# Modulation weights as the stationary operand, and the first weight tile multiplied channel by channel, in the opening of a hybrid diffusion layer

## The chip, the cores and the metric

The kernel runs on one core of one Trainium2 chip. The metric is device time in microseconds (us), from one launch of the whole program. A core has a matrix engine (PE in the profile, with its weight loads shown apart as PEld), a vector engine (DVE), a scalar engine (ACT), GpSimd (POOL), and SyncE (SP), which here only starts transfers.

## The reference, cut to what matters

The layer has 256 context tokens and 2048 latent tokens of 1024 channels. Only its first step matters here:

```python
ml = split_mod(jax.nn.silu(c) @ w_mod[layer] + b_mod[layer])            # 1 x 1024 @ 1024 x 6144
mc = split_mod(jax.nn.silu(c_ctx)[None] @ w_mod[layer] + b_mod[layer])
hl = modulate(rmsnorm(xl, g_norm1[layer]), ml[0], ml[1])                # h * (1 + scale) + shift
hc = modulate(rmsnorm(xc, g_norm1[layer]), mc[0], mc[1])
pl = split_proj(hl @ w_in[layer])                                       # 1024 x 3600
pc = split_proj(hc @ w_in[layer])
```

So a shift and a scale for each of 1024 channels, for two conditioning vectors, must exist before any token can be projected. After that come a bidirectional mLSTM and a short convolution over the tokens, an output projection, a routed mixture of 16 experts, and a final norm.

## The kernel before

The kernel works through the latent tokens in four blocks of 512. For each block it normalises and modulates the tokens, transposes them so that channels lie on the 128 partitions (eight channel groups, k = 0 to 7), and multiplies by `w_in` in tiles of 256 columns. Every projected value is made of three products, because weights and tokens are split into a rounded high part and a low remainder: high times high, high weight times low token, low weight times high token.

The opening is what comes before the first weight tile can be multiplied. Its parts, by name and line:

- **The queue of loads.** Lines 209 to 236 start the loads, most of them on SP's queue, which keeps their order. `wm_load(q)` (L219) brings quarter q of the shift and scale columns of `w_mod`: two tiles of 1 MiB, r = 0 for shift and r = 1 for scale. The order is quarter 0, two context tiles (`cxt`, 512 KiB each), quarter 1, two token tiles (`xt`, 512 KiB each), quarter 2, two token tiles, quarter 3. Behind them come the weight tiles of `w_in`, started by `load_w` (L84). Three loads go by POOL's queue: `gbb`, `ghb` (L131, L133) and `wg` (L276).
- **Buffers.** The quarters 1 to 3 lie in the three `whi` and three `wlo` buffers (pool `whip`) which later hold the split weights. Quarter 0 lies in one `wraw` buffer and in the buffer of `KT`. `split_w` (L89) makes the high part on ACT (L93, `whi`) and the low part on DVE (L97, `wlo`).
- **The modulation** (L248 to L267). For each quarter and each r, eight k-steps multiply the two conditioning vectors `lc` (stationary, 128x2) by 256 columns of `wm` (moving) into `pr` (L255). In the profile each float32 product is two PE instructions, here called passes. DVE copies the two rows out (L257, `mrow`), and two small transposes (L259) put them on partitions in `pm`. Three DVE instructions (L261 to L265) make `B1` and `A1`.
- **Token preparation.** `prep_x` (L154) normalises a tile; `prep_k` (L170) transposes channel group k of all tiles of a set (L176, `pt`), and ACT and DVE make its high and low parts `hhi` and `hlo` (L183 to L187). In the loop over quarters the context runs with quarter q and the tokens one quarter behind.
- **The first products.** `wstat` (L411) multiplies one half of a weight tile (i = 0 or 1) by all eight k into one PSUM bank (`ps`, L417 to L419). The first tile of `w_in` is that of columns 2048 to 2303 (here called tile 1), the next one tile 2; both serve the keys, for the context (256 columns moving) and for the first block (512 columns moving). Results are copied by ACT into `KTc` (L555) and `KT` (L558). PSUM pools: `pmm` has four banks, `ptr` two, `psm` two.

The order on each engine is not the program's: a planner with its own timeline and costs places the instructions of each engine, and the engine then runs its own list strictly in that order.

Of the kernel before, what the change touches and what calls it, by code (L numbers as in the profile page):

```python
# [8 lines left out]
F32 = mybir.dt.float32  # L9
# [10 lines left out]
P = 128  # L20
D = 1024
KD = D // P
SEQ = 2048
NCTX = 256
# [14 lines left out]
def kernel(ctx, tc, x, c, cx, c_ctx, w_mod, b_mod, g_norm1, g_norm2, w_in, w_out, conv_w, conv_b,  # L39
                       gate_b, g_head, w_router, w_gate_e, w_up_e, w_down_e, g_final, out):  # L40
    nc = tc.nc
    V, S, G, T = nc.vector, nc.scalar, nc.gpsimd, nc.tensor
# [3 lines left out]
    w_in = w_in[0]  # L46
# [16 lines left out]
    ident = con.tile([P, P], F32, name="ident")  # L63
# [20 lines left out]
    def load_w(src, rows, cols):  # L84
        raw = wrawp.tile([P, rows, cols], F32, name="wraw", tag="wraw")
        nc.sync.dma_start(raw, src)
        return raw

    def split_w(raw, rows, cols, after=None, after_lo=None):  # L89
        hi = whip.tile([P, rows, cols], F32R, name="whi", tag="whi")  # L90
        if after is not None:
            S.activation(hi[:, 0, 0:1], after, AF.Copy)
        S.activation(hi, raw, AF.Copy)  # L93
        lo = whip.tile([P, rows, cols], F32R, name="wlo", tag="wlo")
        if after_lo is not None:
            tc.keep_in_program_order(G.tensor_copy(lo[:, 0, 0:1], after_lo))
        V.tensor_sub(lo, raw, hi.bitcast(F32))  # L97
        return hi, lo

    vcol = con.tile([P, 96], F32, name="vcol")  # L100
    lc = con.tile([P, KD, 2], F32, name="lc")
# [26 lines left out]
    MB = con.tile([P, NCH + 1, NH], F32, name="MB")  # L128
    Cb0 = con.tile([P, NH, P + 1], F32, name="Cb0")
    gbb = con.tile([P, 16], F32, name="gbb")  # L130
    nc.gpsimd.dma_start(gbb, gate_b.rearrange("o a b -> o (a b)").broadcast_to([P, 16]))  # L131
    ghb = con.tile([P, 512], F32, name="ghb")
    nc.gpsimd.dma_start(ghb, g_head.rearrange("o a b -> o (a b)").broadcast_to([P, 512]))  # L133

    low = ghb[:, 0:2 * P]
    top = ghb[:, 2 * P:3 * P].bitcast(I16)
# [7 lines left out]
    def pool(st, name, bufs, **kw):  # L144
        return st.enter_context(tc.tile_pool(name=name, bufs=bufs, reuse_waits="tile", **kw))

    hp = pool(left, "hT", 12)
    wl = pool(left, "p1l", 2)
    pmm = pool(left, "p1mm", 4, space=PSUM)
    wk = pool(right, "p1e", 2, side="right")  # L150
# [19 lines left out]
    def prep_k(xn, k, s, h, st):  # L170
        his, los = h
        nt = len(xn)
        ntok = nt * P
        pt = ptr.tile([P, 512], F32, name="pt", tag="tr")
        for t in range(nt):
            T.transpose(pt[:, t * P:(t + 1) * P], xn[t][:, k * P:(k + 1) * P], ident)  # L176
        if ntok == 512 or k % 2 == 0:
            st[0] = hp.tile([P, 512], F32R, name="hhi", tag="hhi")
            st[1] = hp.tile([P, 512], F32R, name="hlo", tag="hlo")
        o_ = 0 if ntok == 512 else (k % 2) * ntok  # L180
        hi = st[0][:, o_:o_ + ntok]
        lo = st[1][:, o_:o_ + ntok]
        S.activation(hi, pt[:, :ntok], AF.Identity, scale=A1[:, k, s:s + 1], bias=B1[:, k, s:s + 1])  # L183
        hf = wl.tile([P, 512], F32, name="hf", bufs=2)
        V.tensor_scalar(hf[:, :ntok], pt[:, :ntok], A1[:, k, s:s + 1], B1[:, k, s:s + 1],
                        op0=ALU.mult, op1=ALU.add)
        V.tensor_sub(lo, hf[:, :ntok], hi.bitcast(F32))  # L187
        his.append(hi)
        los.append(lo)
# [9 lines left out]
    wms = []  # L199
# [19 lines left out]
    def wm_load(q):  # L219
        for r in range(2):  # L220
            o_ = r * D + q * 256
            nc.sync.dma_start(wms[q * 2 + r], w_mod[:, o_:o_ + 256].rearrange("(k p) n -> p k n", p=P))

    wm_load(0)
    cxt = [ml2b, ml5b]
    for t in range(2):
        nc.sync.dma_start(cxt[t], cx[t * P:(t + 1) * P, :])
    wm_load(1)
    xn = []
    for t in range(4):  # L230
        xt = wk.tile([P, D], F32, name="xt", bufs=4)
        nc.sync.dma_start(xt, x[t * P:(t + 1) * P, :])
        xn.append(xt)
        if t == 1:
            wm_load(2)
    wm_load(3)
    lcr = wk.tile([16, P], F32, name="lcr", tag="Kt", bufs=2)
    S.activation(lcr, vrow[0:16, :], AF.Silu)
    pv = psm.tile([P, 512], F32, name="pv", tag="sm")
# [6 lines left out]
    prep_x(None, 4, xn)  # L246
    hc, stc = ([], []), [None, None]
    h, sth = ([], []), [None, None]  # L248
    for q in range(4):
        pmf = psm.tile([P, 512], F32, name="pm", tag="sm")  # L250
        pm = pmf[:, 0:8].rearrange("p (r i s) -> p r i s", r=2, i=2)
        for r in range(2):
            pr = pmm.tile([P, 512], F32, name="pr", tag="mm")
            for k in range(KD):
                T.matmul(pr[:2, :256], lc[:, k, :], wms[q * 2 + r][:, k, :], start=k == 0, stop=k == KD - 1)  # L255
            mrow = wk.tile([2, 256], F32, name="mrow", tag="cm" if r else "ur", bufs=1)
            V.tensor_copy(mrow, pr[:2, :256])  # L257
            for i in range(2):
                T.transpose(pm[:, r, i], mrow[:, i * P:(i + 1) * P], ident[:2, :2])  # L259
        sl = slice(q * 2, q * 2 + 2)  # L260
        V.tensor_tensor(B1[:, sl], pm[:, 0], vcol[:, 16 + q * 2:18 + q * 2].unsqueeze(2).to_broadcast([P, 2, 2]),  # L261
                        op=ALU.add)
        V.tensor_tensor(A1[:, sl], pm[:, 1], vcol[:, 24 + q * 2:26 + q * 2].unsqueeze(2).to_broadcast([P, 2, 2]),
                        op=ALU.add)
        V.scalar_tensor_tensor(A1[:, sl], A1[:, sl], 1.0,  # L265
                               vcol[:, 64 + q * 2:66 + q * 2].unsqueeze(2).to_broadcast([P, 2, 2]),
                               op0=ALU.add, op1=ALU.mult)  # L267
        for k in (q * 2, q * 2 + 1):
            prep_k(cxn, k, 1, hc, stc)
        if q:  # L270
            for k in (q * 2 - 2, q * 2 - 1):
                prep_k(xn, k, 0, h, sth)
    for k in range(6, KD):
        prep_k(xn, k, 0, h, sth)
    wg = wl.tile([P, KD, 16], F32, name="wg", bufs=1)
    nc.gpsimd.dma_start(wg, w_in[:, 3584:3600].rearrange("(k p) n -> p k n", p=P))  # L276
    wgp = wl.tile([P, 2, KD, 32], F32R, name="wgp", bufs=1)
    zr = wl.tile([P, KD, 16], F32, name="zr", bufs=1)
    V.memset(zr, 0.0)
# [127 lines left out]
    def wtile(n0):  # L407
        raw = load_w(w_in[:, n0:n0 + 256].rearrange("(k p) n -> p k n", p=P), KD, 256)
        return split_w(raw, KD, 256)

    def wstat(w, i, h, ntok):  # L411
        hi, lo = w
        his, los = h
        ps = pmm.tile([P, 512], F32, name="ps", tag="mm")
        for k in range(KD):
            wh = hi[:, k, i * P:(i + 1) * P]
            T.matmul(ps[:, :ntok], wh, his[k], start=k == 0, stop=False)  # L417
            T.matmul(ps[:, :ntok], wh, los[k], start=False, stop=False)  # L418
            T.matmul(ps[:, :ntok], lo[:, k, i * P:(i + 1) * P], his[k], start=False, stop=k == KD - 1)  # L419
        return ps  # L420
# [127 lines left out]
    for blk in range(4):  # L548
        KT = wk.tile([P, NH, 512], F32, name="KT", bufs=1)
        for j in range(2):  # L550
            w = wtile(2048 + j * 256)
            if blk == 0:
                for i in range(2):
                    ps = wstat(w, i, hc, NCTX)
                    S.activation(KTc[:, j * 2 + i, :], ps[:, :NCTX], AF.Copy)  # L555
            for i in range(2):
                ps = wstat(w, i, h, 512)
                S.activation(KT[:, j * 2 + i, :], ps, AF.Copy)  # L558
        if blk == 0:
            pv = psm.tile([P, 512], F32, name="pv", tag="sm")  # L560
# [3 lines left out]
        for j in range(2):  # L564
            w = wtile(2560 + j * 256)
            if blk == 0:
                for t in range(2):
                    ps = hstat(w, hc, t)
                    V.tensor_copy(V1c[t][:, j * 2:j * 2 + 2, 0:P], ps[:, :256].rearrange("p (h v) -> p h v", h=2))
            for t in range(4):  # L570
                if j == 0:
                    V.memset(V1s[t][:, :, P:P + 1], 1.0)
                ps = hstat(w, h, t)
# [8 lines left out]
        for j in range(2):  # L582
            w = wtile(1536 + j * 256)
            for i in range(2):
                ps = wstat(w, i, h, 512)
# [60 lines left out]
        for j in range(2):  # L646
            mod_tile(j)
            w = wtile(3072 + j * 256)
            for t in range(4):
                so = wl.tile([P, 256], F32, name="so", bufs=2)  # L650
                ps = hstat(w, h, t)
# [4 lines left out]
        for j in range(2):  # L656
            mod_tile(2 + j)
            cs = []
            w = wtile(512 + j * 256)
            for i in range(2):  # L660
                ps = wstat(w, i, h, 512)
# [3 lines left out]
            w = wtile(1024 + j * 256)  # L665
            ys = []
            for i in range(2):
                ct = j * 2 + i
                ps = wstat(w, i, h, 512)
# [11 lines left out]
            w = wtile(j * 256)  # L681
            for i in range(2):
                ct = j * 2 + i
                y = ys[i]
                ps = wstat(w, i, h, 512)
# [3 lines left out]
        h = hnext  # L689

    left.close()
    wk = pool(left, "p2", 2)
# [137 lines left out]
    for n_, k2 in enumerate((2, 3, 0, 1)):  # L830
        raw = load_w(w_out[k2 * 2 * P:(k2 + 1) * 2 * P, :].rearrange("(k p) n -> p k n", p=P), 2, D)
        if n_ < 3:
            hi = whip.tile([P, 2, D], F32R, name="whi", tag="whi")
            lo = whip.tile([P, 2, D], F32R, name="wlo", tag="wlo")
        else:
            hi = wk.tile([P, 2, D], F32R, name="whi3", bufs=1)
            lo = wk.tile([P, 2, D], F32R, name="wlo3", bufs=1)
# [70 lines left out]
    with tc.tile_pool(name="rt", bufs=1, reuse_waits="tile") as rt, tc.tile_pool(name="rtp", bufs=2, space=PSUM, reuse_waits="tile") as rtp:  # L908
# [82 lines left out]
        r = RB[:, 0].rearrange("p (a q) f -> p a q f", a=2)  # L991
# [5 lines left out]
    with tc.tile_pool(name="xw", bufs=2, reuse_waits="tile") as xraw, tc.tile_pool(name="xh", bufs=2, reuse_waits="tile") as xhi, \  # L997
# [159 lines left out]
        for e in range(NE):  # L1157
# [4 lines left out]
            for pr in range(npair):  # L1162
                n = 2 if pr < npair - 1 else NFT - 2 * (npair - 1)
# [22 lines left out]
                for i in range(n):  # L1186
                    ps = pmm.tile([P, 2, 2 * P], F32, name="psx", tag="mm")
                    for m_ in range(2):
                        hi, lo = ws[m_]
                        for k in range(KD):  # L1190
                            wh = hi[:, k, i * P:(i + 1) * P]
# [85 lines left out]
```

## Time and profile before

| what | value |
|---|---|
| median of 3 runs | 2697.55 us (2696.11 to 2704.61) |
| the profiled execution, its own time | 2698.35 us |
| its span, first to last instruction | 2696.3 us |
| PE busy | 2615.3 us, 97% of the span |
| PEld busy | 2365.0 us, 88% |
| DVE busy | 1584.3 us, 59% |
| ACT busy | 1155.3 us, 43% |

The span lies 2.05 us under the time of its own execution, and that time 0.8 us over the median of the runs. Busy time of PE is modelled at its ends and overlaps; the distance from one PE start to the next tells more.

### The profile page before, as it was taken

To read this page: it belongs to the slowest core of one execution; us is meant where nothing else is said; L and a number is where in the kernel's file an instruction comes from. 1 tells how busy PE (TensorE), PEld (TensorE's weight loads), DVE (VectorE), ACT (ScalarE), POOL (GpSimd) and SP (SyncE) were. 2 spreads that over 40 slices of the span, in tenths; PEclk is the share of its full clock that TensorE was granted. 3 is DMA by queue.
4 is the path that set the end of the run, shared out by engine and by line. 5 is a ranking of instruction groups with operands and counts; after the bars stand their busy time and mean duration, and the time that the engine had idled before them with its cause. 6 is when DMAs were issued, how large, how long until landed. Compare 5 with 4: busy or idle time off the path is not lost.

```text
span 2696.3 us, 42922 instructions
## 1 busy us (share of the span) xinstructions
PE 2615.3 (97%) x17570; PEld 2365.0 (88%) x17570; DVE 1584.3 (59%) x2570; ACT 1155.3 (43%) x1723; POOL 301.0 (11%) x345
## 2 busy tenths in 40 slices
PE   8999999999999999689999999999999999999997
PEld 4988888888878888579999999999999999999987
DVE  5356454554575665566566556656655665665684
ACT  3243333422534444354444444444444444444553
POOL 1010000000111111210011011001101100110231
PEclk9999999999999999889999999999999999999999
DMA  8444554645656655165666666666666666666894
GB/s 271 135 147 148 170 165 147 196 129 156 204 183 206 208 183 172 64 219 188 205 217 208 200 209 219 189 208 214 209 202 208 219 191 206 214 210 202 276 318 166
DMA packets 382532, 524.57 MB, mean 195 GB/s; under 512 B 15072, under 2 KB 322736, under 8 KB 380288
## 3 DMA queue, kind: packets, MB, share of 16 engines
q1 hardware_dynamic: 327968, 437.96, 50.0%
q10 hardware_dynamic: 43792, 46.55, 5.1%
q0 software_dynamic: 10576, 37.32, 5.0%
q8 instruction: 138, 2.26, 0.3%
q14 instruction: 58, 0.48, 0.1%
HBM read 449.05 MB, written 72.61 MB: 193 GB/s over the span
## 4 chain that ended last, share of the span: by engine, by line
PE 63%; DMA 3%; DVE 2%; issue 2%; ACT 0%; POOL 0%; POOLq 0%; DVEq 0%; SPq 0%; ACTq 0%
PE psx L1192 12%; PE psx L1194 11%; PE psx L1193 11%; PE ac L1117 6%; PE ac L1119 6%; PE ac L1118 6%; PE po L730 2%; PE po L732 2%; PE po L731 2%; DMA pk<-PK 1%; PE ptx L1055 1%; PE pl L766 1%; PE pb L514 1%; PE pa L510 1%; DMA ACC<-yv,idx 1%
## 5 line engine op out<-in xcount | busy, mean ns | idle before, releaser
L1192 PE MATMUL psx<-xh,whi 128*128 128x256 f32 x2816 | 788.9, 281 | 1.6 <-ACT whi L93 1.5
L1193 PE MATMUL psx<-xl,whi 128*128 128x256 f32 x2816 | 786.7, 280 | 0.9 <-DVE xl L1064 0.9
L1194 PE MATMUL psx<-xh,wlo 128*128 128x256 f32 x2816 | 787.5, 280 | 0.0
L97 DVE TENSOR_TENSOR wlo<-wraw,whi 128x2048 fp32r<-128x2048 f32 x248 | 532.0, 2156 | 307.8 <-ACT whi L93 304.7
L93 ACT ACTIVATE whi<-wraw 128x2048 fp32r<-128x2048 f32 x248 | 446.7, 1804 | 373.3 <-PE psx L1193 112.1
L1194 PEld LDWEIGHTS psx<-xh,wlo 128*128 128x128 f32 x2816 | 535.3, 190 | 0.1
L1193 PEld LDWEIGHTS psx<-xl,whi 128*128 128x128 f32 x2816 | 530.5, 188 | 3.3 <-DVE xl L1064 1.4
L1192 PEld LDWEIGHTS psx<-xh,whi 128*128 128x128 f32 x2816 | 528.7, 188 | 4.1 <-ACT whi L93 1.7
L1117 PE MATMUL ac<-dhi,hh 128*128 128x512 f32 x704 | 276.2, 392 | 0.0
L1118 PE MATMUL ac<-dlo,hh 128*128 128x512 f32 x704 | 274.7, 390 | 0.0
L1119 PE MATMUL ac<-dhi,hl 128*128 128x512 f32 x704 | 273.3, 390 | 0.0
L1077 DVE TENSOR_TENSOR dlo<-draw,dhi 128x2048 fp32r<-128x2048 f32 x96 | 202.9, 2114 | 114.2 <-ACT dhi L1075 114.2
L418 PE MATMUL ps<-hlo,whi 128*128 128x512 f32 (+1 forms) x672 | 259.6, 387 | 0.0
L419 PE MATMUL ps<-hhi,wlo 128*128 128x512 f32 (+1 forms) x672 | 259.0, 386 | 0.0
L417 PE MATMUL ps<-hhi,whi 128*128 128x512 f32 (+1 forms) x672 | 258.6, 388 | 0.0
L1147 POOL DMA_INDIRECT ACC<-yv,idx x28 | 82.8, 2956 | 1124.1 <-DVE yv L1142 1012.6
L1075 ACT ACTIVATE dhi<-draw 128x2048 fp32r<-128x2048 f32 x96 | 170.2, 1772 | 69.7 <-PE ac L1119 67.6
L1201 ACT ACTIVATE hh<-sgt 128x256 fp32r<-128x256 f32 x176 | 73.2, 417 | 263.0 <-DVE sgt L1197 263.0
L1196 ACT ACTIVATE sgt<-psx 128x256 f32<-128x256 f32 x176 | 65.4, 372 | 228.0 <-PE psx L1194 227.9
L1119 PEld LDWEIGHTS ac<-dhi,hl 128*128 128x128 f32 x704 | 132.1, 188 | 27.8
L428 PE MATMUL ps<-whi,hhi 128*128 128x256 f32 x544 | 156.0, 287 | 0.0
L429 PE MATMUL ps<-wlo,hhi 128*128 128x256 f32 x544 | 154.9, 285 | 0.0
(411 smaller groups left out, 3901.8 us busy)
## 6 DMA issues: line engine op xcount, KB each, us to landing
wraw<-in_w_gate_e_dram SPq DMA_DIRECT2D x80, 1024.0 KB, 6.2
wraw<-in_w_up_e_dram SPq DMA_DIRECT2D x80, 1024.0 KB, 5.5
draw<-in_w_down_e_dram SPq DMA_DIRECT2D x80, 1024.0 KB, 6.1
wraw<-in_w_in_dram SPq DMA_DIRECT2D x56, 1024.0 KB, 5.5
pk<-PK SPq DMA_DIRECT2D x16, 1284.0 KB, 7.7
xt<-in_x_dram SPq DMA_DIRECT2D x32, 512.0 KB, 5.5
wraw<-in_w_mod_dram SPq DMA_DIRECT2D x16, 1024.0 KB, 6.8
wm<-in_w_mod_dram SPq DMA_DIRECT2D x8, 1024.0 KB, 12.0
```

The lines of the kernel that those rows point to most:

```text
L93: S.activation(hi, raw, AF.Copy)
L97: V.tensor_sub(lo, raw, hi.bitcast(F32))
L417: T.matmul(ps[:, :ntok], wh, his[k], start=k == 0, stop=False)
L418: T.matmul(ps[:, :ntok], wh, los[k], start=False, stop=False)
L419: T.matmul(ps[:, :ntok], lo[:, k, i * P:(i + 1) * P], his[k], start=False, stop=k == KD - 1)
L1077: V.tensor_sub(lo, raw, hi.bitcast(F32))
L1117: T.matmul(ac, hhs, dh[:, i, sl], start=f == 0, stop=False)
L1118: T.matmul(ac, hhs, dl[:, i, sl], start=False, stop=False)
L1119: T.matmul(ac, hls, dh[:, i, sl], start=False, stop=f == NFT - 1)
L1192: T.matmul(ps[:, m_], wh, xh[:, k], start=k == 0, stop=False)
L1193: T.matmul(ps[:, m_], wh, xl[:, k], start=False, stop=False)
L1194: T.matmul(ps[:, m_], lo[:, k, i * P:(i + 1) * P], xh[:, k], start=False, stop=k == KD - 1)
```

## The change

The quarter's products swap operands: 128 columns of `wm` become the stationary operand and the two vectors of `lc` the moving one, so that the result lands on partitions in `pm` at once; `pr`, the copies `mrow` and the small transposes go away. The order of the loads becomes quarters 0 and 1, context, all four token tiles, weight tile 1 (`raw0`), quarters 2 and 3, then `wg`, `gbb` and `ghb` on SP's queue. Four PSUM banks are held from the opening on for tile 1, two for the context and two for the tokens. Once quarter 1 is done, tile 1 is split, and for every channel group k that is prepared `k0_step(k)` adds twelve products to the four banks. Context and tokens are now prepared together. Where tile 1 was multiplied before, the finished banks are only copied out.

```diff
-    nc.gpsimd.dma_start(gbb, gate_b.rearrange("o a b -> o (a b)").broadcast_to([P, 16]))
-    nc.gpsimd.dma_start(ghb, g_head.rearrange("o a b -> o (a b)").broadcast_to([P, 512]))
...
     wm_load(0)
+    wm_load(1)
     cxt = [ml2b, ml5b]
...
-    wm_load(1)
...
-        if t == 1:
-            wm_load(2)
+    raw0 = load_w(w_in[:, 2048:2304].rearrange("(k p) n -> p k n", p=P), KD, 256)
+    wm_load(2)
     wm_load(3)
+    wg = wl.tile([P, KD, 16], F32, name="wg", bufs=1)
+    nc.sync.dma_start(wg, w_in[:, 3584:3600].rearrange("(k p) n -> p k n", p=P))
+    nc.sync.dma_start(gbb, gate_b.rearrange("o a b -> o (a b)").broadcast_to([P, 16]))
+    nc.sync.dma_start(ghb, g_head.rearrange("o a b -> o (a b)").broadcast_to([P, 512]))
...
+    w0 = None
+    k0c = [pmm.tile([P, 512], F32, name="ps", tag="mm") for _ in range(2)]
+    k0m = [pmm.tile([P, 512], F32, name="ps", tag="mm") for _ in range(2)]
+
+    def k0_step(k):
+        hi, lo = w0
+        for i in range(2):
+            wh = hi[:, k, i * P:(i + 1) * P]
+            wlo_ = lo[:, k, i * P:(i + 1) * P]
+            for ps, (his, los), n in ((k0c[i], hc, NCTX), (k0m[i], h, 512)):
+                T.matmul(ps[:, :n], wh, his[k], start=k == 0, stop=False)
+                T.matmul(ps[:, :n], wh, los[k], start=False, stop=False)
+                T.matmul(ps[:, :n], wlo_, his[k], start=False, stop=k == KD - 1)
...
-            pr = pmm.tile([P, 512], F32, name="pr", tag="mm")
-            for k in range(KD):
-                T.matmul(pr[:2, :256], lc[:, k, :], wms[q * 2 + r][:, k, :], start=k == 0, stop=k == KD - 1)
-            mrow = wk.tile([2, 256], F32, name="mrow", tag="cm" if r else "ur", bufs=1)
-            V.tensor_copy(mrow, pr[:2, :256])
             for i in range(2):
-                T.transpose(pm[:, r, i], mrow[:, i * P:(i + 1) * P], ident[:2, :2])
+                for k in range(KD):
+                    T.matmul(pm[:, r, i], wms[q * 2 + r][:, k, i * P:(i + 1) * P], lc[:, k, :],
+                             start=k == 0, stop=k == KD - 1)
...
-        for k in (q * 2, q * 2 + 1):
+        if q == 0:
+            continue
+        if q == 1:
+            w0 = split_w(raw0, KD, 256)
+        for k in range(0 if q == 1 else q * 2, q * 2 + 2):
             prep_k(cxn, k, 1, hc, stc)
-        if q:
-            for k in (q * 2 - 2, q * 2 - 1):
-                prep_k(xn, k, 0, h, sth)
-    for k in range(6, KD):
-        prep_k(xn, k, 0, h, sth)
-    wg = wl.tile([P, KD, 16], F32, name="wg", bufs=1)
-    nc.gpsimd.dma_start(wg, w_in[:, 3584:3600].rearrange("(k p) n -> p k n", p=P))
+            prep_k(xn, k, 0, h, sth)
+            k0_step(k)
...
-            w = wtile(2048 + j * 256)
+            at0 = blk == 0 and j == 0
+            w = None if at0 else wtile(2048 + j * 256)
...
-                    ps = wstat(w, i, hc, NCTX)
+                    ps = k0c[i] if at0 else wstat(w, i, hc, NCTX)
...
-                ps = wstat(w, i, h, 512)
+                ps = k0m[i] if at0 else wstat(w, i, h, 512)
```

## Rows read from the trace of the kernel before

**Rows 1.** The page: PE's busy time, and the chain that ended last by engine.

```profile
PE 2615.3 (97%) x17570; PEld 2365.0 (88%) x17570; DVE 1584.3 (59%) x2570; ACT 1155.3 (43%) x1723; POOL 301.0 (11%) x345
...
PE 63%; DMA 3%; DVE 2%; issue 2%; ACT 0%; POOL 0%; POOLq 0%; DVEq 0%; SPq 0%; ACTq 0%
```

**Rows 2.** Busy time by stretch: length, engines (instructions), granted clock, DMA share, GB/s.

```profile
9.40:18.40 9.00, 8.95 (x33) 3.08 (x33) 1.17 (x2) 2.30 (x4) 1.35 (x4) 1.00 1.08 344
18.40:46.80 28.40, 27.03 (x139) 11.92 (x139) 15.86 (x42) 10.88 (x18) 4.08 (x9) 1.00 0.97 324
46.80:84.90 38.10, 38.10 (x231) 33.46 (x230) 20.03 (x27) 17.84 (x23) 1.73 (x4) 1.00 0.44 139
```

**Rows 3.** Timeline of PE in the opening: start, length of the group, what, count.

```profile
9.45 8.99 PE L255 MATMUL pr<-wm,lc 128*2 128x256 f32 x32 [4.35 <-DMA wm<-in_w_mod_dram]
...
19.87 3.62 PE L255 MATMUL pr<-wm,lc 128*2 128x256 f32 x16
...
48.86 0.28 PE L417 MATMUL ps<-hhi,whi 128*128 128x256 f32 x1
48.98 0.28 PE L418 MATMUL ps<-hlo,whi 128*128 128x256 f32 x1
...
53.93 0.39 PE L417 MATMUL ps<-hhi,whi 128*128 128x512 f32 x1
54.16 0.39 PE L418 MATMUL ps<-hlo,whi 128*128 128x512 f32 x1
```

**Rows 4.** Groups by line and shape, first 60 us: busy us, mean ns.

```profile
L255 PE MATMUL pr<-wm,lc 128*2 128x256 f32 x128 | 30.7, 397 | 4.9 <-DMA wm<-in_w_mod_dram 4.9
...
L97 DVE TENSOR_TENSOR wlo<-wraw,whi 128x2048 fp32r<-128x2048 f32 x3 | 6.8, 2278 | 0.6 <-ACT whi L93 0.6
L93 ACT ACTIVATE whi<-wraw 128x2048 fp32r<-128x2048 f32 x3 | 5.7, 1914 | 1.2 <-DMA wraw<-in_w_in_dram 1.2
...
L185 DVE TENSOR_SCALAR hf<-pt,A,B 128x512 f32<-128x512 f32 x6 | 4.6, 802 | 2.2 <-ACT hhi L183 2.2
...
L257 DVE COPY mrow<-pr 2x256 f32<-2x256 f32 x8 | 3.3, 409 | 16.5 <-PE pr L255 16.5
...
L259 PE MATMUL pm<-ident,mrow 2*128 2x2 f32 x16 | 2.2, 207 | 0.0
```

**Rows 5.** Timeline of ACT: first token tile, tile 1's split, tile 2's last copy.

```profile
23.77 1.06 ACT L165 ACTIVATE xq<-xt 128x1024 bf16<-128x1024 f32 x1 [6.14 <-DMA xt<-in_x_dram]
...
44.02 1.91 ACT L93 ACTIVATE whi<-wraw 128x2048 fp32r<-128x2048 f32 x1 [0.94 <-DMA wraw<-in_w_in_dram]
...
85.07 0.58 ACT L558 ACTIVATE KT<-ps 128x512 f32<-128x512 f32 x1
```

**Rows 6.** Float32 weights of 128 columns with few columns moving: one line, one timeline group.

```profile
L643 PE MATMUL pq<-ones,macc x32: 164/250/251, 332.4 to 573.2; 128*128 128x1 f32 x32
...
1112.53 0.97 PEld L766 LDWEIGHTS pl<-wra,xT 128*128 128x128 f32 x8
```

**Rows 7.** Timeline of the weight loads before the clock rose, and at the low clock.

```profile
4.50 0.18 PEld L240 LDWEIGHTS pv<-ident,lcr 16*128 16x128 f32 x1 [4.50 <-POOL Tb L70]
4.72 0.18 PEld L243 LDWEIGHTS pv<-ident,vrow 72*128 72x128 f32 x1
...
794.27 1.83 PEld L498 LDWEIGHTS pP<-pk 128*128 128x128 f32 x8
```

**Rows 8.** Stretches around the clock's changes, columns as in rows 2.

```profile
788.20:791.60 3.40, 0.57 (x6) 0.38 (x4) 2.54 (x2) 1.01 (x1) 0.00 (x0) 1.00 0.31 96
791.60:795.00 3.40, 2.39 (x11) 2.40 (x12) 3.40 (x4) 0.90 (x4) 0.00 (x0) 0.50 0.72 222
...
1115.90:1119.30 3.40, 2.21 (x17) 1.77 (x15) 1.65 (x6) 0.00 (x0) 1.29 (x3) 1.00 0.38 154
1119.30:1122.70 3.40, 0.59 (x2) 0.17 (x2) 2.22 (x15) 0.80 (x3) 3.21 (x5) 0.50 0.06 22
```

**Rows 9.** Transfers started in the first 150 us: KB, us to landing.

```profile
ghb<-in_g_head_dram POOLq DMA_DIRECT2D x1, 256.0 KB, 8.7
```

**Rows 10.** Timeline of PE: bfloat16 weights of 128 columns, four columns moving.

```profile
1156.29 1.15 PE L1013 MATMUL pi<-Cb,oh 128*128 128x4 bf16 x16 [2.02 <-DVE Cb L994]
```

## The prediction

> **What bounds the kernel now.** I read the page first: PE is busy 97% of the span and leads the chain that ended last; no other engine or queue has more than 3% of it [rows 1]. A change of 8 us (0.3% of 2697.55, about what a measurement of this kernel can tell from no change) must therefore show up as PE time or PE idle time. Next, the opening in stretches [rows 2]. What the reader is to see is that PE is already full there: busy 8.95 of 9.00 us, then 27.03 of 28.40, then all of 38.10. The DMA queues are full as well until 46.8 us, but PE does not stand waiting for them; the idle time is 1.4 us in all after the first modulation matmul at 9.45 [rows 3]. So the opening is no hole that work can be moved into. What counts is how much PE work it holds, at which clock, and whether the new order makes PE wait where it does not now.
>
> My finish line is the end of tile 2, PE time 84.9 [rows 2, 5]. Until then 16 matmuls of the tile after it have slipped in, 0.12 us each, so the line is 83.0 in equal work.
>
> **The change part by part.**
>
> *Modulation.* Removed: 128 passes with 256 columns moving. Sixteen of them take 3.62 us, and less one modelled tail of 0.38 this is 0.216 us each, 27.6 us together [rows 3, 4]. The first ones ran at the low clock: 32 took 8.99 us where 7.1 would be due, so about 2 us lost [rows 3] (the clock column reads 1.00 there [rows 2], the spacing says otherwise). Removed too: sixteen small transposes at 0.11 us, 1.8 us of PE, and eight DVE copies of 0.41 us, 3.3 us, on an engine with room (59% busy) [rows 1, 4]. Added: 4 quarters x 2 x 2 halves x 8 k = 128 products, and since float32 takes two passes a product (16 products of L643 are 32 instructions [rows 6]), 256 passes with a weight load of 128x128 each and only two columns moving. The nearest row is the router's, 16 columns moving: eight loads in 0.97 us, less one length of 0.19, 0.112 us a pass [rows 6]. So 28.7 us: halving the price and doubling the count cancel. At the full clock PE saves 27.6 + 1.8 - 28.7 = 0.7 us. This is the heart of the forecast: no PE work is saved.
>
> *The clock of these passes.* At the low level (1.2 GHz) eight loads take 1.83 us, less a length of 0.33, 0.214 each; two loads before the clock first rose, one with 16 columns moving, stand 0.216 apart [rows 7]. So a pass costs 0.112 at 2.4 GHz and 0.216 at 1.2. Which applies? The kernel starts at the low level, and before, ten back-to-back 256-column passes came ahead of the rise. No row shows a long stream of loads with two columns moving. The nearest is 1115.9 to 1119.3: eight such loads, two transposes and a tail of dense matmuls, PE busy 2.21 of 3.40 us, and the clock fell after it [rows 8]. Before the fall at 791.6 PE had been busy only 0.57 us [rows 8]. I take the low level for quarters 0 and 1, because they start low and nothing dense comes before them. Bounds: 256 passes at 0.112 (28.7 us) and at 0.216 (55.3 us).
>
> By the Trainium skill, page "TensorE: Matmul & The Clock Gate", section "LDWEIGHTS (loading the stationary operand)", a load takes its columns divided by 1.2 GHz, 107 ns for 128, with no clock in the rule. At the full clock the row agrees (112 ns); at the low one it does not (214 ns). By the rule the modulation would be 27.4 us at either clock, and the case would end as the first rival below.
>
> *Order of loads.* From the first token tile's landing at 23.77 to tile 1's at 44.02, 6.5 MiB came: 3.1 us each [rows 5]. Now tile 1 stands 2.5 MiB behind that tile's old place: 31.5, less about 1 us for the small loads moved behind, so 30.5; quarter 2 is complete at 36.7 and quarter 3 at 42.9. Tile 1's high part takes 1.91 us on ACT, so products can start at 32.4 at the earliest; the low part is 2.28 us of DVE behind it [rows 4]. But both need buffers that quarter 1 holds: the high part waits for its r = 0 passes, the low part for r = 1. Queued behind these splits are the `hhi` and `hf` preparations, and PE's products wait for them.
>
> *Tile 1 channel by channel.* Same 96 products as before: 48 at 0.12 and 48 at 0.23, 16.7 us [rows 3]; they move ahead, nothing is saved. Four `pmm` banks are held, but `pr` no longer wants one. Copying out costs ACT 0.58 us for 512 columns [rows 5], hidden behind the other three banks' last products; uncovered it is 0.6 us. Preparing k = 6 and 7 after quarter 3 hides behind the products of k = 4 and 5 (4.2 us) if they are still there; a DVE step is 0.80 us [rows 4], and I take 1.0 us of wait, between 0 and 2.5.
>
> *The three moved loads* stand on SP ahead of tile 2's load. The biggest, `ghb`, took 8.7 us to land [rows 9]. Tile 2 would land before 55, and is wanted after 69 in every case below: free; without that cover up to 9 us.
>
> **The sum.** Quarters 0 and 1 from 9.4: 128 passes x 0.216 = 27.6, to 37.0. Then 24 transposes for k = 0 to 3 (eight context, sixteen token) at 0.214, 5.1, to 42.1. Left are tile 1 (16.7), quarters 2 and 3 at the full clock between dense products (14.3), 24 transposes at 0.11 (2.6), a low start of the products as in the old opening (2.1), the wait (1.0): 36.7, to 78.8. Tile 2: 95.5. Against 83.0 this is +12.5 us. On the profiled execution: span 2696.3 plus 12.5, plus 2.05 outside it, 2710.9; on the median of the runs, 0.8 lower, 2710. Everything behind is PE's, so the shift stays to the end.
>
> **The rivals.**
>
> *The clock rises during the stream of loads.* Then quarters 0 and 1 end at 9.4 + 2.1 + 14.3 = 25.8, and PE waits for tile 1: products from 32.4, the same 36.7 us behind, 69.1, tile 2 at 85.8: +2.8, 2700 us. For it: the loads keep PE's weight path full. Against it: the fall at 1119.3. This is the case of no measurable change. It decides where both quarters and the 24 transposes (2.6) end before 32.4, that is at under 0.16 us a pass. The rule named above would end here too.
>
> *The change does what it says and the passes are cheaper than the router's.* The cheapest row of a 128-column load is bfloat16: 16 in 1.15 us, 0.063 each [rows 10]. Then the last two quarters cost 8.1 instead of 14.3, and tile 2 ends at 79.6: -3.4, 2694 us. Against it: both float32 rows. Even so it is within 0.3%.
>
> *Quarters 2 and 3 run low as well,* because the planner lays their passes in one piece: another 128 x 0.104 = 13.3 us, +26, 2723. For it: 64 passes of a quarter come ready together. This is the far end of the forecast's own case.
>
> *The planner orders something else anew,* here (a pass of quarter 2 ahead of the first products holds PE from 32.4 to 36.7, 4.3 us) or later, with either sign.
>
> **How the numbers follow.** Low clock in quarters 0 and 1, with or without part of 2 and 3: 0.56, of which 0.48 above +8.1 us; it ends lower when only quarter 0 is low (+6). Clock rises: 0.28, of which 0.25 within 0.3%, 0.03 slower by an added wait. Cheaper passes: 0.08, half of it beyond -8 with some luck in the loads. New order elsewhere: 0.08, faster 0.04, same 0.02, slower 0.02. Faster 0.08, same 0.39, slower 0.53. The likeliest is 2710, its own range 2703 to 2722. The range of all reaches to the cheap passes below and to half of the low quarters 2 and 3 above: 2695 to 2720.
>
> **What would show it.** L255's successor: 256 PE instructions; their distance in quarter 0 and 1 near 0.216 (right) or 0.112 (first rival). The first product near 40, not 32. Tile 2's last copy (L558, 85.07 before [rows 5]) near 97 if right, 88 if the clock rises. The granted clock at 0.5 in stretches up to some 45 us. Wrong would be: the passes under 0.1 us, PE standing idle for quarter 2 or 3, or a shift at tile 2 that is gone by the end.

## The result and the profile after

The changed kernel takes 2717.49 us (median of 5 runs, 2715.21 to 2726.89), 1.0069 times the kernel before, interval 1.0052 to 1.0086: slower by 0.5 to 0.9%. The forecast was 2710, its own range 2703 to 2722. The profiled execution took 2720.44 us, with a span of 2718.7. Of the runs in the table below, one of 3225.15 and one of 3260.12 us, at granted clocks of 0.758 and 0.747, count in no ratio.

From the page: PE's busy time grew by 22.2 us and the span by 22.4, and PE leads the chain as before [rows 1]. DVE and ACT did not move.

```profile
PE 2637.5 (97%) x17682; PEld 2405.7 (88%) x17682; DVE 1583.6 (58%) x2562; ACT 1155.6 (43%) x1723; POOL 300.9 (11%) x342
...
PE 61%; issue 3%; DMA 3%; DVE 2%; ACT 1%; POOL 0%; POOLq 0%; ACTq 0%; SPq 0%; DVEq 0%
```

The timeline of PE in the opening, against [rows 3]:

```profile
7.39 27.44 PE L271 MATMUL pm<-lc,wm 128*128 128x2 f32 x128 [2.41 <-DMA wm<-in_w_mod_dram]
...
36.01 3.84 PE L271 MATMUL pm<-lc,wm 128*128 128x2 f32 x18
39.71 0.56 PE L261 MATMUL ps<-hhi,whi 128*128 128x256 f32 x1
...
45.65 1.18 PE L271 MATMUL pm<-lc,wm 128*128 128x2 f32 x10
...
59.16 4.26 PE L271 MATMUL pm<-lc,wm 128*128 128x2 f32 x20
```

The reader is to divide: 128 passes of quarters 0 and 1 in 27.3 us are 0.21 us each, and so are the twenty at 59.16; the ten at 45.65 stand 0.11 apart. The same instruction costs two prices, and which one it pays is in the granted clock. Stretches cut where the clock changed, columns as in [rows 2] (the clock column reads 1.00 up to the first rise at 45.07, where the spacing shows the low clock):

```profile
7.39:34.70 27.31, 27.31 (x129) 27.31 (x129) 4.85 (x9) 8.80 (x13) 6.39 (x12) 1.00 1.08 366
34.70:45.07 10.37, 10.37 (x46) 9.98 (x47) 6.14 (x13) 1.90 (x3) 0.00 (x0) 1.00 0.96 275
45.07:58.73 13.66, 13.66 (x107) 12.87 (x107) 8.01 (x13) 5.74 (x7) 0.00 (x0) 1.00 0.17 53
58.73:68.97 10.24, 10.24 (x46) 9.75 (x44) 3.80 (x8) 3.35 (x4) 0.00 (x0) 0.50 0.32 102
68.97:72.38 3.41, 3.41 (x31) 3.33 (x31) 0.05 (x1) 0.39 (x1) 0.00 (x0) 1.00 0.02 5
72.38:75.79 3.41, 3.41 (x12) 2.75 (x11) 3.41 (x7) 0.95 (x2) 0.00 (x0) 0.50 0.00 0
...
7.39:99.20 91.81, 91.78 (x497) 86.40 (x498) 35.03 (x62) 30.02 (x43) 8.93 (x16) 0.93 0.60 194
```

PE is busy 91.78 of 91.81 us: nothing waits, and the loss is clock. It is low for 37.7 + 10.2 + 3.4 = 51.3 us; before it was low for the first 3.9 us of the modulation. At half the clock half of that is lost, by an estimate 25.7 us against 2.0. Of the 23.7 us more, the start 2.1 us sooner and the waits that are gone (1.4) take up a part; another 4 us, up to the measured 16.0 below, I did not take apart.

To measure the opening alone I use the first product of the tile behind tile 2. It stands in the timelines of PE, of before and of after, at

```profile
83.28 0.28 PE L428 MATMUL ps<-whi,hhi 128*128 128x256 f32 x1
```

```profile
99.29 0.28 PE L440 MATMUL ps<-whi,hhi 128*128 128x256 f32 x1
```

so +16.0 us, and every PE instruction from there to 305 us is shifted by the same 16.0. Tile 2's last copy moved as far, from 85.07 [rows 5] to

```profile
101.08 0.58 ACT L571 ACTIVATE KT<-ps 128x512 f32<-128x512 f32 x1
```

The span grew by 6.4 us more than that; where these come from is taken up below.

### The profile page after: what moved, and what is told of

The parts are those of the page before. It is cut to its first block, busy times and chain, and to the rows that moved or that the text cites. A ratio compares the mean times of both kernels' runs of the same rounds, so it can differ in the third digit from the quotient of the medians.

```text
span 2718.7 us, 43139 instructions
## 1 busy us (share of the span) xinstructions
PE 2637.5 (97%) x17682; PEld 2405.7 (88%) x17682; DVE 1583.6 (58%) x2562; ACT 1155.6 (43%) x1723; POOL 300.9 (11%) x342
## 4 chain that ended last, share of the span: by engine, by line
PE 61%; issue 3%; DMA 3%; DVE 2%; ACT 1%; POOL 0%; POOLq 0%; ACTq 0%; SPq 0%; DVEq 0%
PE psx L1205 11%; PE psx L1207 11%; PE psx L1206 11%; PE ac L1132 6%; PE ac L1130 6%; PE ac L1131 6%; PE po L743 2%; PE po L745 2%; PE po L744 2%; DMA pk<-PK 1%; PE ptx L1068 1%; PE pl L779 1%; PE pb L526 1%; PE pa L522 1%; DMA ACC<-yv,idx 1%
## 5 line engine op out<-in xcount | busy, mean ns | idle before, releaser
L430 PE MATMUL ps<-hlo,whi 128*128 128x512 f32 (+1 forms) x640 | 249.4, 390 | 0.0
L429 PE MATMUL ps<-hhi,whi 128*128 128x512 f32 (+1 forms) x640 | 249.1, 391 | 0.0
L431 PE MATMUL ps<-hhi,wlo 128*128 128x512 f32 (+1 forms) x640 | 249.1, 390 | 0.0
```

## The experiments

"Shift" is the start of that first product behind tile 2 less 83.28 us, from one profile each. In every kernel here PE's instructions from there to 305 us come in the same order and all have that shift, to 0.03 us; how much it differs between executions of one kernel was not measured. Medians of the kernel before, taken at different times, differ by 3.6 us. Each ratio is to runs of the kernel before taken beside it, with medians of 2697.55 us (first row), 2700.77 (rows 2 to 5), 2701.14 (rows 6 to 9) and 2701.06 (last two); it is not quite the ratio of the two medians.

| kernel | shift, us | median, us | ratio to before (95%) |
|---|---|---|---|
| changed kernel | +16.0 | 2717.49 | 1.0069 (1.0052 to 1.0086) |
| changed, 120 columns moving | +4.8 | 2710.99 | 1.0043 (1.0029 to 1.0057) |
| changed, old operands | +11.3 | 2719.39 | 1.0065 (1.0052 to 1.0079) |
| before, operand swap alone | +24.6 | 2727.04 | 1.0101 (1.0085 to 1.0116) |
| before, swap, 120 columns | -0.2 | 2702.06 | 1.0002 (0.9993 to 1.0011) |
| changed, dense products first | +8.0 | 2715.68 | 1.0049 (1.0031 to 1.0068) |
| before, three loads moved | -1.6 | 2701.78 | 0.9998 (0.9989 to 1.0007) |
| the same, dense products first | -2.6 | 2700.40 | 0.9997 (0.9988 to 1.0006) |
| before, new order of loads | +2.2 | 2703.30 | 1.0010 (1.0000 to 1.0020) |
| before, swap, 120 columns, loads moved, dense first | -2.4 | 2698.94 | 0.9997 (0.9987 to 1.0006) |
| changed, 120 columns, dense first, gap filled | +1.6 | 2707.15 | 1.0020 (1.0011 to 1.0030) |

### One part at a time: operands and order

The first four kernels cross the two halves of the change (operands; order of loads with channel-by-channel products) and add a third form of the operands, with more columns moving over the same weight loads:

```diff
-        pm = pmf[:, 0:8].rearrange("p (r i s) -> p r i s", r=2, i=2)
+        pm = pmf[:, 0:480].rearrange("p (r i s) -> p r i s", r=2, i=2)
...
-                    T.matmul(pm[:, r, i], wms[q * 2 + r][:, k, i * P:(i + 1) * P], lc[:, k, :],
+                    T.matmul(pm[:, r, i].rearrange("p (a s) -> p a s", s=2),
+                             wms[q * 2 + r][:, k, i * P:(i + 1) * P],
+                             lc[:, k, :].unsqueeze(1).to_broadcast([P, 60, 2]),
```

(`A1` and `B1` read the first two of the 120 result columns.)

**The changed kernel with 120 columns.** 

> The changed kernel with one difference: each modulation pass has 120 columns moving instead of two (the two vectors repeated 60 times; only the first two result columns are used). Same 256 passes with the same 128x128 weight loads, same order of loads, same channel-by-channel products. Theory (the passes with two columns moving leave the granted clock at 1.2 GHz, and what is lost is the modulation's): the clock rises early in quarter 0, most passes stand about 0.112 us apart instead of 0.216, the first tile-1 product starts near 32 us instead of 39.7, and of the 16 us at the end of tile 2 some 12 go: about 2703 us against 2717.5. Rival A (the new order of loads and the channel-by-channel products cost the time): 2717, no change from the changed kernel. Rival B (a 128x128 float32 load takes 0.216 us at this place whatever moves with it): 2717 as well, with the passes still 0.216 us apart.

PE's timeline, then its stretches up to and in the low clock:

```profile
7.03 16.16 PE L271 MATMUL pm<-lc,wm 128*128 128x120 f32 x128 [1.90 <-DMA wm<-in_w_mod_dram]
...
29.69 0.58 PE L261 MATMUL ps<-hhi,whi 128*128 128x256 f32 x1 [1.13 <-ACT whi L93]
```

```profile
7.03:10.50 3.47, 3.47 (x16) 3.47 (x17) 0.00 (x0) 0.00 (x0) 0.00 (x0) 1.00 1.11 345
10.50:27.50 17.00, 14.12 (x121) 13.26 (x119) 5.51 (x14) 7.80 (x14) 5.48 (x12) 1.00 1.07 376
27.50:34.40 6.90, 5.18 (x20) 4.53 (x21) 4.93 (x6) 2.58 (x2) 0.00 (x0) 0.51 1.10 348
65.10:68.50 3.40, 3.33 (x15) 3.16 (x15) 2.52 (x6) 0.58 (x2) 0.00 (x0) 0.50 0.93 299
```

The same 128 loads take 16.0 us instead of 27.3: the first 16 passes are 0.22 apart, then the clock rises at 10.5 and they stand 0.112 apart. Sixty times the columns, and 11 us less. That ends rival B, and the shift falls by 11.2 us, as the theory had it (12). It does not fall to nothing: 4.8 us are left, and the time, at 1.0043, lies well above the 2703 expected.

**The swap in the kernel before, with two and with 120 columns.** 

> The kernel before with the operand swap alone: 256 passes with two columns moving; order of loads and tile 1 as before. Theory: the passes of quarters 0 and 1 run at 1.2 GHz, 0.216 us apart, and those of quarters 2 and 3 partly; 128 to 192 passes x 0.104 us gives 13 to 20 us, so 2710 to 2717. Rival A: about 2697, as the kernel before. Rival B: 256 x 0.216 against 29.4 us before, some 26 us less what hides in waits for loads, 2715 to 2723.

> The kernel before with the operand swap, and 120 columns moving in each pass instead of two. Theory: the clock rises early in quarter 0 as before, the passes stand 0.112 us apart, and the time is that of the kernel before within 3 us, 2694 to 2701. Rival A: about 2697 too. Rival B: 2715 to 2723.

The modulation of the first in PE's timeline, and its stretch up to the first rise of the clock (before it, the column reads 1.00):

```profile
9.34 13.79 PE L255 MATMUL pm<-lc,wm 128*128 128x2 f32 x64 [4.32 <-DMA wm<-in_w_mod_dram]
...
23.87 13.65 PE L255 MATMUL pm<-lc,wm 128*128 128x2 f32 x64
...
63.12 6.40 PE L255 MATMUL pm<-lc,wm 128*128 128x2 f32 x30
```

```profile
9.34:75.20 65.86, 65.86 (x312) 65.86 (x313) 24.93 (x48) 19.04 (x27) 4.69 (x12) 1.00 0.70 227
```

And that of the second, with its stretch up to the rise and the whole of its opening:

```profile
9.36 9.84 PE L255 MATMUL pm<-lc,wm 128*128 128x120 f32 x64 [4.11 <-DMA wm<-in_w_mod_dram]
...
19.78 3.73 PE L255 MATMUL pm<-lc,wm 128*128 128x120 f32 x32
```

```profile
9.36:14.53 5.17, 5.17 (x24) 5.17 (x25) 0.00 (x0) 0.00 (x0) 0.00 (x0) 1.00 1.08 334
9.36:83.11 73.75, 71.06 (x498) 65.93 (x499) 34.51 (x62) 29.48 (x44) 6.37 (x16) 1.00 0.73 239
```

With two columns PE is busy for 65.86 of 65.86 us, loading weights all the time, and the clock does not leave 1.2 GHz before the dense products have begun at 70. All 256 passes cost 53.9 us, against 30.2 for the 128 of before: +23.7, nearly the whole shift of 24.6 and near the far rival's +26. Expected were 13 to 20: I had let the clock rise within quarters 2 and 3. With 120 columns the shift is -0.2. So with the clock up the swap gains next to nothing in all, as the sum had it (0.7 us): PE's work shrinks by 1.4 us (71.06 busy, 72.46 before), and its waits grow by 1.3. With two columns moving, the same loads cost 24.8 us more, and PE does not wait at all. The profile's busy columns do not tell the two apart: ahead of the rise at 14.53 they are as full with 120 columns.

**The changed kernel with the old operands.** The modulation's lines are those of before (128 passes of 256 columns, `mrow`, small transposes), with `pr` in the `ptr` pool, since the `pmm` banks are held. 

> The changed kernel, but with the modulation's operands as before (the two vectors stationary, 256 columns of the modulation weights moving, 128 passes, copies and small transposes); the new order of loads and the channel-by-channel products stay. Theory: the loss was the operand swap's, so the time is about the kernel before, 2694 to 2701 us; the first product waits for tile 1 and starts near 33 us. Rival A (order of loads and channel-by-channel products cost the time): 2712 to 2718. Rival B: about 2697, as the theory.

Theory and measurement part here: +11.3 us, though no pass has two columns; the time of 2719.39 us lies above rival A's range as well. PE's waits from 36 us on, and three rows of its timeline:

```profile
PE ps L261 <- ACT hhi L181: 4.7, 2, 2.3
```

```profile
51.93 0.28 PE L275 MATMUL pm<-ident,mrow 2*128 2x2 f32 x2
...
55.12 0.51 PE L261 MATMUL ps<-hhi,whi 128*128 128x256 f32 x2 [2.33 <-ACT hhi L181]
...
72.03 0.50 PE L261 MATMUL ps<-hhi,whi 128*128 128x256 f32 x2 [2.35 <-ACT hhi L181]
```

From 7.56 to 94.5 us PE is idle for 7.9 us, where it was 1.4 before: 4.7 of them behind quarters 2 and 3, where copies, small transposes, `A1` and `hhi` stand one behind the other and PE's list holds nothing to put between. But one DVE instruction stands among them that the quarter does not need: between the copy `mrow` and `B1` and `A1`, DVE's list has the low split of a later weight tile. For quarter 2, from DVE's timeline:

```profile
51.46 0.41 DVE L273 COPY mrow<-pr 2x256 f32<-2x256 f32 x1 [6.71 <-PE pr L271]
51.80 2.27 DVE L97 TENSOR_TENSOR wlo<-wraw,whi 128x2048 fp32r<-128x2048 f32 x1
54.00 0.14 DVE L277 TENSOR_TENSOR B<-pm,vcol 128x4 f32<-128x4 f32 x1
...
54.25 0.16 DVE L281 SCALAR_TENSOR_TENSOR A<-A,vcol 128x4 f32<-128x4 f32 x1
```

The small transposes are done at 52.21, `B1` starts at 54.00: by that, 1.8 of the 2.3 us stand behind the split. For quarter 3 it is the same (split at 68.63, small transposes done at 69.10, `B1` at 70.92). No run put the split behind `A1`, so it is not shown how much of the waits would then go. And from 29.9 to 36.7 the clock is low. So rival A is partly right: the new order, as the planner laid it out, has a price of its own. The two halves of the change do not add: alone they shift by 24.6 and 11.3 us, together by 16.0. Slow passes fill the gaps which faster ones leave open: in the changed kernel PE waits for nothing, with 120 columns it is idle for 6.3 us (from 7.03 to 88.03).

### Is it the low start, or the passes?

The prediction took the low clock for quarters 0 and 1 "because they start low and nothing dense comes before them". This kernel puts something dense before them:

```diff
+    pd = ptr.tile([P, 512], F32, name="pd", tag="tr")
+    for _ in range(4):
+        T.matmul(pd[:, :256], ones, sg, start=True, stop=True)
...
+    for _ in range(4):
+        T.matmul(pd[:, :216], ones, vcol[:, :72].unsqueeze(1).to_broadcast([P, 3, 72]), start=True, stop=True)
     cxn = prep_x(None, 2, cxt)
```

> The changed kernel with eight dense float32 products ahead of quarter 0 (four of 256 columns, four of 216; their result is not used), in the time in which PE otherwise waits for the first modulation weights. Theory S (the prediction's reason: quarters 0 and 1 are slow because the kernel starts at the low clock and nothing dense stands before them): the clock is up when quarter 0 starts and stays up, the passes stand 0.112 us apart, the two quarters take 14.3 us instead of 27.4, the first tile-1 product starts near 31 us instead of 39.7, and the shift of what comes after tile 2 falls from 16.0 us to about 4. Theory P (the stream of two-column passes itself lets the clock fall): the granted clock rises in the dense products and falls again within quarter 0, most passes stand 0.216 apart, and the shift stays at 12 to 15 us, the time at 2713 to 2717 on the scale of the changed kernel's 2717.

PE's timeline, and stretches cut at the clock's rise and fall:

```profile
6.04 1.73 PE L251 MATMUL pd<-vcol,ones 128*128 128x216 f32 x8 [0.32 <-DVE vcol L249]
7.86 22.95 PE L276 MATMUL pm<-lc,wm 128*128 128x2 f32 x128
...
35.69 0.56 PE L266 MATMUL ps<-hhi,whi 128*128 128x256 f32 x1
```

```profile
6.00:12.82 6.82, 6.69 (x53) 6.38 (x53) 0.00 (x0) 0.00 (x0) 0.00 (x0) 1.00 1.10 348
12.82:40.12 27.30, 27.30 (x127) 27.10 (x128) 9.47 (x17) 10.71 (x16) 6.16 (x12) 0.50 1.07 350
```

The clock is up at 6.00, ahead of quarter 0, and falls at 12.82 while PE does nothing but two-column passes; 44 of them ran at 0.112, the other 84 at 0.213, and it stays low to 40.12. That is theory P's picture: the stream does not only fail to raise the clock, it loses it. The shift is neither theory's, though: 8.0, not 4 and not 12 to 15. (The time, 2715.68 us, does lie in theory P's range, but some 6.5 us of it lie behind the opening.) Quarters 0 and 1 give 4.5 us (22.8 instead of 27.3). The rest came with the second part: in quarters 2 and 3 the clock, once up at 40.12, did not fall again before tile 2's end, while in the changed kernel it was low for another 13.7 us there. The planner mixed passes and products there a little differently (the longest run of passes is 14 in this kernel, 20 in the changed one); whether that decided it, these runs don't tell.

### The order of the loads

Three kernels in the frame of the one before, with the old operands. First the three loads `wg`, `gbb`, `ghb` alone, put on SP's queue behind quarter 3. 

> The kernel before, with only the three loads (gates, head norm, gate weights) taken from POOL's queue and put behind the last modulation quarter on SP's queue, as the change does. If they delayed the first weights, quarter 0 starts near 7.4 us instead of 9.45. If PE's work sets the opening, what comes after tile 2 moves 1.5 to 2 us ahead; if the landing of quarter 3 and of tile 1 sets it, it moves by less than 0.5 us. The time is within 2 us of the kernel before either way.

Then the dense products as well. 

> As the run with the three loads moved, and the eight dense products ahead of quarter 0. The low start of the modulation (32 passes in 8.99 us where 7.1 are due) goes, so quarter 0 ends another 1.5 to 2 us sooner; what comes after tile 2 moves ahead by as much if PE's work sets the opening (3 to 4 us ahead of the kernel before in all), or not at all if loads set it.

Then the whole new order of loads, and nothing else of the change. 

> The kernel before with the whole new order of loads (quarters 0 and 1, context, four token tiles, tile 1, quarters 2 and 3, then the three moved loads), but the modulation's operands, the loop over quarters and tile 1 as before. It splits the 11.3 us that the changed kernel with the old operands is behind at the end of tile 2. If the order of loads costs them (tokens come later, PE idles and the clock falls): 5 to 11 us behind the kernel before. If the channel-by-channel products do (a chain of copies, transposes and splits before each quarter's products): between 2 us ahead and 2 us behind.

The first modulation rows of the three, in this order, each a timeline of PE in its own kernel:

```profile
7.57 9.59 PE L257 MATMUL pr<-wm,lc 128*2 128x256 f32 x32 [2.41 <-DMA wm<-in_w_mod_dram]
```

```profile
7.58 7.07 PE L262 MATMUL pr<-wm,lc 128*2 128x256 f32 x32
```

```profile
7.37 9.87 PE L257 MATMUL pr<-wm,lc 128*2 128x256 f32 x38 [2.20 <-DMA wm<-in_w_mod_dram]
...
30.14 5.68 PE L257 MATMUL pr<-wm,lc 128*2 128x256 f32 x16
```

Moving the three loads brings the first weights 1.9 us sooner, and 1.6 of them reach the end of tile 2. The dense products give back the low start (32 passes in 7.07 instead of 9.59), but only 1.0 us of that 2.5 arrives: PE now waits 1.0 us for the context's preparation and 0.4 for a token tile's. The new order of loads costs 2.2 us net of its early start, just outside the nearer of the two ranges: with both quarters first, the tokens come late, the clock falls at 27.5 and sixteen passes of quarter 2 take 5.68 us instead of 3.62. The other 9 us of the old operands' 11.3 come with the new loop and its channel-by-channel products: 5.3 of them are waits (idle for 7.9 us instead of 2.5, most of it shown above), and 3.5 are PE's busy time (79.1 instead of 75.6), which I did not take apart.

### What is left of the new order with the clock kept up

```diff
         if q == 1:
             w0 = split_w(raw0, KD, 256)
+            pmd = psm.tile([P, 512], F32, name="pmd", tag="sm")
+            for k in list(range(KD)) * 3:
+                T.matmul(pmd[:, 0:120].rearrange("p (a s) -> p a s", s=2), wms[1][:, k, 0:P],
+                         lc[:, k, :].unsqueeze(1).to_broadcast([P, 60, 2]), start=True, stop=True)
```

> The changed kernel with 120 columns moving, the eight dense products ahead of quarter 0, and 24 more such products of 120 columns (48 passes, 5.6 us, not used) behind quarter 1, in the gap in which PE otherwise waits for the tokens' preparation and for tile 1. With 120 columns alone the shift after tile 2 was 4.8 us. Theory (PE's gap lets the clock fall, and the fall from 27.5 to 34.4 is what costs): no fall there, and the shift is 0 to 2 us. Rival (the gap itself costs, whatever the clock): 3 to 5 us.

```profile
7.59 14.45 PE L276 MATMUL pm<-lc,wm 128*128 128x120 f32 x128
21.88 5.52 PE L292 MATMUL pmd<-lc,wm 128*128 128x120 f32 x48
```

```profile
21.88:31.18 9.30, 6.78 (x57) 6.18 (x56) 5.18 (x9) 6.97 (x11) 4.77 (x9) 1.00 1.08 357
```

The clock rises at 5.9 and does not fall before 794; the shift is 1.6. So 3.2 of the 4.8 us came back with the clock kept up; as this run takes away the low start and the two falls together, it does not part them. PE is still idle for 2.5 us from 21.88 to 31.18, and work that nobody needs, laid into its waits, paid for itself.

### A version from what spoke for itself

> The kernel before with what the runs so far spoke for: operands swapped with 120 columns moving (no copies, no small transposes), the three loads moved behind quarter 3, and the eight dense products ahead of quarter 0. If PE's work sets the opening, the gains add: about 3 to 5 us ahead of the kernel before after tile 2. If the landing of the modulation quarters sets it (the run with 120 columns waited 1.6 us for quarter 2 already), no more than the 2.6 us of the run with old operands. Of the time, 0.1 to 0.2%, within what a measurement can tell from nothing.

The shift is -2.4, no more than without the swap. PE waits for quarter 2 as foreseen, 1.4 of the 4.3 us that it is idle in this opening (2.3 without the swap):

```profile
25.51 3.38 PE L262 MATMUL pm<-lc,wm 128*128 128x120 f32 x28 [1.43 <-DMA wm<-in_w_mod_dram]
```

Of the time it is 0.9997 (0.9987 to 1.0006). No kernel here beats the one before by what a measurement can tell.

### The rest of the span

The changed kernel's span grew by 6.4 us beyond its opening. From 305 to 728.62 us (times of before) the shift grows by 4.5, although PE's order is the same; 2.8 of this come near 314, where PE waits 1.5 us for `gsb` instead of 0.3 and the clock is low from 331.8 to 335.2 (times of the changed kernel). From there to 1112.53 it grows by another 4.3, and behind that 2.4 are gained back. The middle part is in the planner's lists: from 807 to 1094 us four kernels have the old order on PE (before; both swaps with 120 columns in its frame; the old operands with loads moved and dense products), the others another one. Between the same two instructions in that part, the last `pM` transpose and the last transpose of `xs`, columns as in [rows 2]; from the version above (old order), the one with three loads moved, and the changed kernel:

```profile
726.79:1110.27 383.48, 371.82 (x2212) 324.41 (x2212) 234.44 (x620) 156.20 (x503) 53.94 (x103) 0.99 0.55 186
```

```profile
727.64:1113.39 385.75, 372.35 (x2213) 323.08 (x2212) 236.44 (x620) 155.88 (x503) 56.81 (x103) 1.00 0.55 185
```

```profile
749.12:1137.38 388.26, 374.64 (x2212) 325.51 (x2212) 236.68 (x620) 155.87 (x503) 55.77 (x103) 0.99 0.55 184
```

In the old order the part takes 382.8 to 383.9 us in four profiles, in the other orders 385.7 to 391.1 in eight. PE's busy time is the same 372 in the first two; the idle time is 11.7 and 13.4. The changed kernel's 388.3 also holds a fall of the clock at 1123.7. So I count some 2 to 4 us to the new order. That is argued from these windows: no run changed this order alone. In the times it hardly shows: beyond the shift, and against the median of before beside them, kernels with the old order lost 0.3 to 2 us, those with another 0 to 7. The rest, and why it scatters so, stays open.

## Why the prediction was right, and where it was off

The sign and the mechanism were right. By its own steps:

- **PE is full, so work and clock decide.** Right: 91.78 of 91.81 us busy, and +22.2 us of busy time for +22.4 of span.
- **No PE work is saved.** Right: the swap with 120 columns, in the frame of before, shifts by -0.2 us against a forecast of 0.7 saved; 1.4 us less work there goes into waits.
- **0.112 or 0.216 by the clock.** Right, in one kernel: the twenty passes at 59.16 and the ten at 45.65. By the Trainium skill, "TensorE: Matmul & The Clock Gate", section "LDWEIGHTS (loading the stationary operand)", the modulation would be, by an estimate from its 107 ns a load, 27.4 us at either clock. The traces disagree: 53.9 us where the clock was low throughout.
- **Quarters 0 and 1 low.** Right in size, 27.3 us against 27.6. The reason was half of it: the low start matters (4.5 us), but the stream lost the clock also when it had been raised.
- **Quarters 2 and 3 at the full clock, the products of tile 1 with one low start.** This is the mis-sized term. The passes took 17.7 us where 14.3 stood (45 of the 128 stand 0.213 apart, 9.6 us of it), and tile 1's products 23.4 where 16.7 + 2.1 stood, because the clock rose only at 45.07 and fell again at 58.73 and 72.38. Together +8.0. The nearest row [rows 8] showed such a fall behind router loads, and I used it for the first quarters alone.
- **What made up for it.** The start at 7.39 instead of 9.4 (-2.0; moving the three loads does this, and I had costed it only as a delay of tile 2), no wait for quarter 3 instead of 1.0, and 0.9 less for the transposes. With quarters 0 and 1 0.3 shorter, that makes +8.0 - 4.2 = +3.8 on a forecast of +12.5: 16.3, against a measured 16.0. That the forecast came as near as it did is in part luck, since two misses of opposite sign half cancel.
- **Loads.** Tile 1 was predicted at 30.5. With 120 columns its split starts at 27.73, so it came three us sooner; in the changed kernel the split waits for quarter 1's buffer, as foreseen, and nothing hangs on the landing.
- **Everything behind is PE's, so the shift stays.** Right to 305 us, then not: +6.4 in the profiled execution. In the medians it is +3.9 (19.9 less 16.0), but the interval of the ratio, some 14 to 23 us, holds 16.0 as well. The rival of a new order elsewhere came true beside the forecast, as a small loss if the windows above are read rightly.
- **The rivals.** "The clock rises" was priced at +2.8 us: 120 columns give +4.8, and +1.6 with the clock kept up. "All quarters low" was priced at +26: the swap alone gives +24.6. "Cheaper passes" fell.

## What to carry to other kernels

A PE that the profile calls busy all the time can be working at half its clock: take the distance of instruction starts, and compare it with the same instruction elsewhere. Turning a product so that the short side moves swaps streaming for weight loads; price a long run of such passes at both levels of the clock (here 0.112 and 0.213 us a pass), and do not count on the higher because PE is busy. Two halves of a change need not add: slow work hid the waits which the new order shows with faster passes. Before a wait is put down to a chain of needed steps, look at what else stands in that engine's list between them.

## What the runs showed that I had not expected

- More columns through the same loads made them faster: 128 passes with 2 columns 27.3 us, with 120 columns 16.0.
- 44 two-column passes ran at 2.4 GHz behind dense products; then the granted clock fell, with PE busy without a break, and 84 ran at 1.2 GHz.
- With the old operands a 2.27 us split of a later weight tile stood on DVE ahead of `A1`, and by the rows 1.8 of each wait of 2.3 us lie behind it.
- 5.5 us of products that nobody reads, in a gap of PE, and eight dense ones ahead of the first quarter, brought the rest 3.2 us forward.
